# SSD groups of a hybrid decoder layer: the second state product issued behind the products of y, the transposes back to channels moved into the next group

## The chip, the cores and the metric

The kernel runs on one core of one Trainium2 chip. The metric is the device time of one launch in microseconds (us), given as the median of three runs. Besides it there is one profiled execution, and all shares and rows below are of that one. The engines are named as the profile names them: PE (matrix products and transposes), DVE (vector), ACT (activations, scaled copies), POOL, SP (issues most DMAs). The granted clock of PE was 0.997 of full speed, that is the 2.4 GHz level throughout.

## The reference

One decoder layer over 256 tokens and 2048 channels, all in float32. One projection of the input feeds three token mixers (Mamba-2 SSD, S5, RWKV-7), their gates and the merge gates; the branch outputs are projected, gated, summed, projected once more, and normalized. The change is in the SSD mixer, which has 8 groups of 4 heads and two chunks of 128 tokens:

```python
def ssd_chunked(xh, dt, a, bm, cm):
    x = (xh * dt[..., None]).reshape(b, c, l, g, j, p)
    cs = jnp.cumsum(da, -1)
    lmat = jnp.exp(segsum(da))
    cb = jnp.einsum('bclgn,bcsgn->bcgls', cc, bc)
    y_diag = jnp.einsum('bcgls,bgjcls,bcsgjp->bclgjp', cb, lmat, x)
    decay_states = jnp.exp(cs[..., -1:] - cs)
    states = jnp.einsum('bclgn,bgjcl,bclgjp->bcgjpn', bc, decay_states, x)
    ...
    y_off = jnp.einsum('bclgn,bcgjpn,bgjcl->bclgjp', cc, states, jnp.exp(cs))
    return (y_diag + y_off).reshape(b, s, h, p)

# mamba2_branch, after it
    y = ssd_chunked(xh, dt, a, bm, cm) + d_skip[:, None] * xh
    y = y.reshape(b, s, SSD_WIDTH) * jax.nn.silu(z)
    yg = y.reshape(b, s, SSD_GROUPS, SSD_WIDTH // SSD_GROUPS)
    yg = yg * lax.rsqrt(jnp.mean(jnp.square(yg), -1, keepdims=True) + SSD_NORM_EPS)
    return yg.reshape(b, s, SSD_WIDTH) * norm_w
```

## The kernel before

**Matrix products.** Every large product is made of three passes over a split of both operands (high by high, low by high, high by low). Weights come in halves of 512 KB: SP issues the DMA into a raw buffer (tile `raw_*`, ring of 4, line 338), ACT makes the high half (`hi_*`, ring of 4, L344), DVE subtracts it from the raw one (`lo_*`, ring of 4, L346), and PE runs 24 products on it: L417 to L419 in `proj` (tiles `ps_*`, 3 PSUM buffers with tag "pj"), L863 to L865 for the SSD gate z (tiles `zq`, same 3 buffers), L1234 to L1236 for the branch outputs (`br`).

**Order of the work.** The rows of the program are issued group by group from a list: first the RWKV part (to about 545 us), then the second list, which holds the SSD groups S0 to S7 (about 463 to 843 us, overlapping RWKV's last chunks), between them the tiles s0 to s7 of S5, then the splits of the SSD outputs (step "ah", L424 and L425, tiles `yh0h`, `yh0l`), the branch outputs with their gates (`g0_j` is a gate's projection, `b0_j` the weights of the branch product, `sg` the gate, L1281, L1297), and the output projection. This list is only the order in which instructions are created. A scheduler with a timeline model of its own decides the order in each engine's queue, and the pools hand out their buffers in that order. `high_priority` moves what is created under it ahead; `issue_after(ins)` keeps what is created under it behind `ins` in its engine's queue. Each engine then works its queue strictly in order.

**One SSD group.** Four projections give xs (2), B and C; every second group also makes z for two groups (`zs`, one buffer, tanh on L869 and a product on L870). Two DMAs fetch the cumulated decays for all partitions (`csb0`, `csb1`, line 896; the same ring of 5 buffers holds `xdt` and `y_`). PE makes C by B of both chunks and turns B (`cb`, L902, L903) and xs (`xt`, L912). DVE scales (`xdt` L914, `y` L916, `xdec` L921). PE makes the state of the first chunk (`st`, L924), ACT copies it (`ST`, L926), PE multiplies it by C of the second chunk (L927, the second state product), DVE scales that and adds it to y (L929, L930). Meanwhile ACT and DVE make the decay matrices in place in csb (relu L936, exp L937, times CB L938), and PE makes the products of y (`y`, L942). Then comes the chain to the end of the group: sum (L945), times z (L946), squares (L950), root (L952), reciprocal (L953), scaling (L955), four transposes back to channels on PE (`yT`, L959), and the scaled copies into `ya` (ACT, L961). The tiles `cb`, `xt`, `st`, `y` and `yT` of all groups share two PSUM buffers (tag "s"). `ya` lies in memory that RWKV used, so the first four of these copies are written together at 545 us.

Of the kernel before, what the change touches and what calls it, by code (L numbers as in the profile page):

```python
# [11 lines left out]
ALU = mybir.AluOpType  # L12
# [4 lines left out]
T = 256  # L17
# [187 lines left out]
def emit(tc, I, O, parts=("rwkv", "s5", "ssd", "final"), dbg=None):  # L205
    nc = tc.nc
    ctx = ExitStack()
    with ctx:
# [67 lines left out]
        for st in PROG2:  # L276
            k, n = st[0], st[1:]
            if st == "dt":
                ssd_dt(g)
            elif k == "S":  # L280
                ssd_group(g, int(n))
                if st == "S7":
                    sd.close()
                    g.fp = ctx.enter_context(tc.tile_pool(name="fp", bufs=1, reuse_waits="tile"))
            elif k == "s":
                s5_tile(g, int(n))
            elif k == "z":
                s5_zb(g, int(st[2:]))
            elif st == "ch":
                acts[2] = hilo_in(g, "yh2", g.yc, lambda nm: ych.pop(0), g.ycr)  # L290
            elif st == "ah":
                ring = lambda nm: g.fp.tile([128, T], F32R, name=nm, tag="hl", bufs=31)
                acts[0] = hilo_in(g, "yh0", g.ya, ring, g.yar)
            elif st == "bh":
                s5.close()
                g.op = ctx.enter_context(tc.tile_pool(name="op", bufs=1, reuse_waits="tile"))
                out_setup(g)
                acts[1] = hilo(g, "yh1", [g.yb[:, j, :] for j in range(8)], True)
            elif k in "cab":
                branch(g, "abc".index(k), int(n), acts, wts)  # L300
            elif k == "U":
                s5_glu(g)
            elif k == "G":
                gate_b(g, int(n))
# [484 lines left out]
LC = 128  # L789
# [62 lines left out]
def ssd_z(g, zp):  # L852

    nc = g.nc
    ps = [g.pp.tile([128, 512], F32, name=f"zq{zp}_{tk}", tag="pj", bufs=3) for tk in range(2)]
    for kb in range(4):
        hi, lo = g.loadw(g.I["wza"][4 * zp + kb], f"za{zp}_{kb}")
        for k in range(4):
            kk = 4 * kb + k
            f0, l0 = kk == 0, kk == NK - 1  # L860
            for tk in range(2):
                t = slice(128 * tk, 128 * tk + 128)
                nc.tensor.matmul(ps[tk], lhsT=g.xhi[:, kk, t], rhs=hi.k512(k), start=f0, stop=False)  # L863
                nc.tensor.matmul(ps[tk], lhsT=g.xhi[:, kk, t], rhs=lo.k512(k), start=False, stop=False)  # L864
                nc.tensor.matmul(ps[tk], lhsT=g.xlo[:, kk, t], rhs=hi.k512(k), start=False, stop=l0)  # L865
    g.zs = g.cz(f"zs{zp}")
    with g.tc.high_priority():
        for tk in range(2):
            nc.scalar.activation(g.zs[:, tk, :], ps[tk], AF.Tanh, scale=0.5)  # L869
            nc.vector.scalar_tensor_tensor(g.zs[:, tk, :], g.zs[:, tk, :], 1.0, ps[tk], ALU.add, ALU.mult)  # L870


def ssd_group(g, gr):
    nc, tc = g.nc, g.tc
    cv = []
    for n, t in (("xs0", 2 * gr), ("xs1", 2 * gr + 1), ("B", 16 + gr), ("C", 24 + gr)):
        ps = g.proj(f"x{t}")
        a = g.cv(f"{n}_{gr}")
        with tc.high_priority():
            nc.scalar.activation(a, ps, AF.Identity, scale=g.p("cw", 96 + t), bias=g.p("cb", t))  # L880
            for d in (1, 2, 3):
                nc.vector.scalar_tensor_tensor(a[:, d:T], ps[:, 0:T - d], g.p("cw", 32 * (3 - d) + t), a[:, d:T], ALU.mult, ALU.add)
        th = g.kp.tile([128, T], F32, name=f"th{n}_{gr}", tag="th", bufs=2)
        nc.scalar.activation(th, a, AF.Tanh)
        nc.vector.scalar_tensor_tensor(a, th, 1.0, a, ALU.add, ALU.mult)
        cv.append(a)
    if gr % 2 == 0:
        ssd_z(g, gr // 2)
    zs = g.zs[:, :, 256 * (gr % 2):256 * (gr % 2) + 256]
    xs, B, C = cv[0:2], cv[2], cv[3]  # L890
    idn = g.c("ident")
    hs = slice(4 * gr, 4 * gr + 4)
    csb = []
    for c in range(2):
        t = g.k2(f"csb{c}_{gr}", (128, 4, LC))
        nc.sync.dma_start(t, g.csd[hs, LC * c:LC * c + LC].unsqueeze(0).to_broadcast([128, 4, LC]))
        csb.append(t)

    p1 = g.pp.tile([128, 3, LC], F32, name=f"cb{gr}", tag="s", bufs=2)
    for c in range(2):  # L900
        w = slice(LC * c, LC * c + LC)
        nc.tensor.matmul(p1[:, c, :], lhsT=B[:, w], rhs=C[:, w], start=True, stop=True)  # L902
    nc.tensor.transpose(p1[:, 2, :], B[:, 0:LC], idn)  # L903
    BT = g.k1(f"BT{gr}", (128, LC))
    nc.scalar.activation(BT, p1[:, 2, :], AF.Copy)
    CBm = g.k1(f"CBm{gr}", (128, 2, LC))
    nc.vector.tensor_tensor(CBm, p1[:, 0:2, :], g.c("mC").unsqueeze(1).to_broadcast([128, 2, LC]), ALU.mult)

    p2 = g.pp.tile([128, 2, 4, 64], F32, name=f"xt{gr}", tag="s", bufs=2)
    for c in range(2):  # L910
        for q in range(2):
            nc.tensor.transpose(p2[:, c, 2 * q:2 * q + 2, :].rearrange("p a b -> p (a b)"), xs[q][:, LC * c:LC * c + LC], idn)  # L912
    xdt = g.k2(f"xdt{gr}", (128, 2, 4, 64))
    nc.vector.tensor_tensor(xdt, p2, g.csT[:, 1, :, hs].unsqueeze(3).to_broadcast([128, 2, 4, 64]), ALU.mult)  # L914
    y = g.k2(f"y_{gr}", (128, 2, 4, 64))
    nc.vector.tensor_tensor(y, p2, g.dskb[:, hs].unsqueeze(1).unsqueeze(3).to_broadcast([128, 2, 4, 64]), ALU.mult)  # L916
    dec = g.kp.tile([128, 4], F32, name=f"dec{gr}", tag="dec", bufs=2)
    nc.vector.tensor_tensor(dec, csb[0][:, :, LC - 1], g.csT[:, 0, 0, hs], ALU.subtract)
    nc.scalar.activation(dec, dec, AF.Exp)
    xdec = g.k1(f"xdec{gr}", (128, 4, 64))  # L920
    nc.vector.tensor_tensor(xdec, xdt[:, 0], dec.unsqueeze(2).to_broadcast([128, 4, 64]), ALU.mult)  # L921

    p3 = g.pp.tile([128, 2, T], F32, name=f"st{gr}", tag="s", bufs=2)
    nc.tensor.matmul(p3[:, 0, :], lhsT=BT, rhs=xdec.rearrange("p a b -> p (a b)"), start=True, stop=True)  # L924
    ST = g.k1(f"ST{gr}")
    nc.scalar.activation(ST, p3[:, 0, :], AF.Copy)  # L926
    nc.tensor.matmul(p3[:, 1, :], lhsT=C[:, LC:T], rhs=ST, start=True, stop=True)  # L927
    off = g.k1(f"off{gr}", (128, 4, 64))
    nc.vector.tensor_tensor(off, p3[:, 1, :].rearrange("p (a b) -> p a b", a=4), g.ecs[:, hs].unsqueeze(2).to_broadcast([128, 4, 64]), ALU.mult)  # L929
    nc.vector.tensor_tensor(y[:, 1], y[:, 1], off, ALU.add)  # L930

    M = csb
    for c in range(2):
        E = csb[c]
        for h in range(4):
            nc.scalar.activation(E[:, h, :], E[:, h, :], AF.Relu, scale=-1.0, bias=g.csT[:, 0, c, 4 * gr + h:4 * gr + h + 1])  # L936
        nc.scalar.activation(E, E, AF.Exp, scale=-1.0)  # L937
        nc.vector.tensor_tensor(E, E, CBm[:, c, :].unsqueeze(1).to_broadcast([128, 4, LC]), ALU.mult)  # L938
    p4 = g.pp.tile([128, 2, 4, 64], F32, name=f"y{gr}", tag="s", bufs=2)
    for c in range(2):  # L940
        for h in range(4):
            nc.tensor.matmul(p4[:, c, h, :], lhsT=M[c][:, h, :], rhs=xdt[:, c, h, :], start=True, stop=True)  # L942

    y = y.rearrange("p c a b -> p c (a b)")
    nc.vector.tensor_tensor(y, y, p4.rearrange("p c a b -> p c (a b)"), ALU.add)  # L945
    nc.vector.tensor_tensor(y, y, zs, ALU.mult)  # L946
    ss = g.kp.tile([128, 2], F32, name=f"ss{gr}", tag="ss", bufs=2)
    sq = g.k1(f"sq{gr}")
    for c in range(2):
        nc.scalar.activation(sq, y[:, c, :], AF.Square, accum_out=ss[:, c:c + 1])  # L950
    rs = g.kp.tile([128, 2], F32, name=f"rs{gr}", tag="rs", bufs=2)
    nc.scalar.activation(rs, ss, AF.Sqrt, scale=1.0 / 256, bias=g.ssdeps)  # L952
    nc.vector.reciprocal(rs, rs)  # L953
    for c in range(2):
        nc.scalar.activation(y[:, c, :], y[:, c, :], AF.Identity, scale=rs[:, c:c + 1])  # L955
    p6 = g.pp.tile([128, 2, T], F32, name=f"yT{gr}", tag="s", bufs=2)
    for q in range(2):
        for c in range(2):
            nc.tensor.transpose(p6[:, q, LC * c:LC * c + LC], y[:, c, 128 * q:128 * q + 128], idn)  # L959
    for q in range(2):  # L960
        nc.scalar.activation(g.ya[2 * gr + q], p6[:, q, :], AF.Identity, scale=g.p("nw", 2 * gr + q))  # L961

# [427 lines left out]
```

## Time and profile before

| what | value |
|---|---|
| median of 3 runs | 1308.43 us (1305.89 to 1310.21) |
| profiled execution | 1302.54 us, its span 1300.6 us |
| granted clock of PE | 0.997 |
| PE busy | 1268.7 us (98%) |
| DVE busy | 995.7 us (77%) |
| ACT busy | 768.5 us (59%) |
| bytes moved | 230.71 MB, 177 GB/s |

The span is the time from the first to the last instruction of the profiled execution; 1.9 us of its run lie outside. A wait is idle time of an engine just before an instruction, put down to what released it. Where PE is busy nearly all the time, what it waits for is what can be gained, and every new wait of PE is lost.

### The profile page before, as it was taken

The page shows a single profiled execution, that of the slowest core. Times are in us where ns is not written, and L with a number is a line of the kernel's source. Part 1 is how long each engine was busy: PE and PEld are TensorE (multiplying, and loading weights), DVE is VectorE, ACT ScalarE, POOL GpSimd, SP SyncE. Part 2 cuts the span into 40 slices and gives each one's busy share as a digit, 9 for nine tenths or more (in the row PEclk, how much of TensorE's full clock was granted, in tenths as well). Part 3 has the DMA queues.
Part 4 walks back from the last instruction along what each step waited for, and adds up shares of the span by engine and source line. Part 5 has one row for each costly group of instructions (what it writes and reads, how often), then busy time and mean ns, then how long its engine had stood idle before and what let it go on. Part 6 is the DMA issues. An engine that isn't in the chain of part 4 may idle for free.

```text
span 1300.6 us, 27378 instructions
## 1 busy us (share of the span) xinstructions
PE 1268.7 (98%) x10916; PEld 1195.2 (92%) x10916; DVE 995.7 (77%) x1823; ACT 768.5 (59%) x1379; POOL 14.8 (1%) x72
## 2 busy tenths in 40 slices
PE   8999999999999999989999999999999999999996
PEld 8999999999989889889989989999999999999885
DVE  6779987669959857889999867999597565448655
ACT  6676555577555657885756766766454454444530
POOL 2000000000000000000000000000000000000000
PEclk9999999999999999999999999999999999999998
DMA  8655655444564554555555556456655656677751
GB/s 313 181 169 173 187 174 167 139 124 145 166 177 152 168 183 132 159 186 164 178 163 180 170 178 195 146 158 192 193 171 164 193 179 211 209 230 243 255 167 65
DMA packets 97039, 230.71 MB, mean 177 GB/s; under 512 B 26736, under 2 KB 41616, under 8 KB 96912
## 3 DMA queue, kind: packets, MB, share of 16 engines
q1 hardware_dynamic: 96336, 227.60, 57.1%
q8 instruction: 86, 1.41, 0.5%
q10 hardware_dynamic: 576, 1.36, 0.3%
q14 instruction: 41, 0.34, 0.1%
HBM read 224.37 MB, written 3.24 MB: 175 GB/s over the span
## 4 chain that ended last, share of the span: by engine, by line
PE 80%; DVE 7%; ACT 6%; DMA 3%; issue 2%; SPq 1%; DVEq 0%; POOL 0%; ACTq 0%; POOLq 0%
PE ps_g L418 6%; PE ps_g L417 6%; PE ps_g L419 6%; PE br L1235 4%; PE br L1234 4%; PE br L1236 4%; PE ps_x L417 3%; PE ps_x L418 3%; PE ps_x L419 3%; PE po L1337 2%; PE po L1338 2%; PE po L1339 2%; PE zq L865 2%; PE zq L864 2%; PE zq L863 2%
## 5 line engine op out<-in xcount | busy, mean ns | idle before, releaser
L417 PE MATMUL ps_g<-xhi,hi_g 128*128 128x256 f32 x768 | 215.2, 280 | 0.0
L418 PE MATMUL ps_g<-xlo,hi_g 128*128 128x256 f32 x768 | 215.1, 280 | 0.0
L419 PE MATMUL ps_g<-xhi,lo_g 128*128 128x256 f32 x768 | 213.8, 278 | 0.0
L346 DVE TENSOR_TENSOR lo_g<-raw_g,hi_g 128x1024 fp32r<-128x1024 f32 x96 | 117.5, 1224 | 66.6 <-ACT hi_g L344 61.9
L344 ACT ACTIVATE hi_g<-raw_g 128x1024 fp32r<-128x1024 f32 x96 | 101.5, 1058 | 93.8 <-PE ps_g L418 71.4
L418 PEld LDWEIGHTS ps_g<-xlo,hi_g 128*128 128x128 f32 x768 | 144.6, 188 | 2.0 <-issue 1.0
L417 PEld LDWEIGHTS ps_g<-xhi,hi_g 128*128 128x128 f32 x768 | 144.6, 188 | 0.9
L417 PE MATMUL ps_x<-xhi,hi_x 128*128 128x256 f32 x512 | 144.6, 282 | 0.6 <-ACT sq L950 0.6
L419 PEld LDWEIGHTS ps_g<-xhi,lo_g 128*128 128x128 f32 x768 | 144.2, 188 | 0.5
L418 PE MATMUL ps_x<-xlo,hi_x 128*128 128x256 f32 x512 | 143.9, 281 | 0.0
L419 PE MATMUL ps_x<-xhi,lo_x 128*128 128x256 f32 x512 | 143.6, 280 | 0.0
L344 ACT ACTIVATE hi_b<-raw_b 128x1024 fp32r<-128x1024 f32 x64 | 67.8, 1059 | 75.8 <-PE br L1235 43.9
L346 DVE TENSOR_TENSOR lo_x<-raw_x,hi_x 128x1024 fp32r<-128x1024 f32 x64 | 78.3, 1223 | 27.1 <-ACT hi_x L344 27.1
L417 PEld LDWEIGHTS ps_x<-xhi,hi_x 128*128 128x128 f32 x512 | 96.3, 188 | 1.6 <-ACT sq L950 0.8
L419 PEld LDWEIGHTS ps_x<-xhi,lo_x 128*128 128x128 f32 x512 | 96.3, 188 | 0.9 <-issue 0.2
L418 PEld LDWEIGHTS ps_x<-xlo,hi_x 128*128 128x128 f32 x512 | 96.3, 188 | 0.7 <-issue 0.2
L346 DVE TENSOR_TENSOR lo_b<-raw_b,hi_b 128x1024 fp32r<-128x1024 f32 x64 | 78.8, 1231 | 21.6 <-ACT hi_b L344 19.6
L344 ACT ACTIVATE hi_x<-raw_x 128x1024 fp32r<-128x1024 f32 x64 | 67.5, 1055 | 39.7 <-PE ps_x L418 23.2
L1234 PE MATMUL br<-yh0h,hi_b 128*128 128x256 f32 x256 | 72.0, 281 | 0.7 <-DVE sg L1297 0.7
L1235 PE MATMUL br<-yh0l,hi_b 128*128 128x256 f32 x256 | 72.3, 283 | 0.0
L1236 PE MATMUL br<-yh0h,lo_b 128*128 128x256 f32 x256 | 71.7, 280 | 0.0
L676 DVE TENSOR_TENSOR Pm<-TT,AT 128x16 f32<-128x16 f32 (+30 forms) x124 | 50.8, 410 | 11.6 <-POOL AT L672 5.8
(446 smaller groups left out, 3872.9 us busy)
## 6 DMA issues: line engine op xcount, KB each, us to landing
raw_g<-in_wt SPq DMA_DIRECT2D x96, 512.0 KB, 4.4
raw_x<-in_wt SPq DMA_DIRECT2D x64, 512.0 KB, 4.2
raw_za<-in_wza SPq DMA_DIRECT2D x32, 512.0 KB, 3.8
raw_b<-in_wba SPq DMA_DIRECT2D x32, 512.0 KB, 4.5
raw_wo<-in_wout SPq DMA_DIRECT2D x32, 512.0 KB, 4.7
raw_k<-in_wt SPq DMA_DIRECT2D x16, 512.0 KB, 4.8
raw_r<-in_wt SPq DMA_DIRECT2D x16, 512.0 KB, 4.1
raw_v<-in_wt SPq DMA_DIRECT2D x16, 512.0 KB, 3.8
```

The lines of the kernel that those rows point to most:

```text
L344: nc.scalar.activation(hi, raw, AF.Copy)
L346: nc.vector.tensor_tensor(lo, raw, hi.bitcast(F32), ALU.subtract)
L417: m.append(nc.tensor.matmul(ps, lhsT=hi.k(k), rhs=g.xhi[:, k, :], start=(k == 0), stop=False))
L418: m.append(nc.tensor.matmul(ps, lhsT=hi.k(k), rhs=g.xlo[:, k, :], start=False, stop=False))
L419: m.append(nc.tensor.matmul(ps, lhsT=lo.k(k), rhs=g.xhi[:, k, :], start=False, stop=(k == NK - 1)))
L676: nc.vector.tensor_tensor(Pm[:, :, 0:n], TT[:, :, 0:n], col, ALU.mult)
L863: nc.tensor.matmul(ps[tk], lhsT=g.xhi[:, kk, t], rhs=hi.k512(k), start=f0, stop=False)
L864: nc.tensor.matmul(ps[tk], lhsT=g.xhi[:, kk, t], rhs=lo.k512(k), start=False, stop=False)
L865: nc.tensor.matmul(ps[tk], lhsT=g.xlo[:, kk, t], rhs=hi.k512(k), start=False, stop=l0)
L1234: nc.tensor.matmul(ps, lhsT=hi.k(k0 + k), rhs=h, start=(k == 0), stop=False)
L1235: nc.tensor.matmul(ps, lhsT=hi.k(k0 + k), rhs=l, start=False, stop=False)
L1236: nc.tensor.matmul(ps, lhsT=lo.k(k0 + k), rhs=h, start=False, stop=(k == n - 1))
```

## The change

The second state product and the two DVE steps after it are created after the products of y, and the product is kept behind the last of them in PE's queue. The transposes back to channels, with the copies into `ya`, become a function of their own, `ssd_back`. Groups 0 to 6 store it, and the next group calls it right after its transpose of B is created; its transposes are kept behind that instruction in PE's queue. Group 7 calls it at once.

```diff
-    nc.tensor.transpose(p1[:, 2, :], B[:, 0:LC], idn)
+    m = nc.tensor.transpose(p1[:, 2, :], B[:, 0:LC], idn)
+    if gr:
+        g.late(m.ins)
     BT = g.k1(f"BT{gr}", (128, LC))
...
     ST = g.k1(f"ST{gr}")
     nc.scalar.activation(ST, p3[:, 0, :], AF.Copy)
-    nc.tensor.matmul(p3[:, 1, :], lhsT=C[:, LC:T], rhs=ST, start=True, stop=True)
-    off = g.k1(f"off{gr}", (128, 4, 64))
-    nc.vector.tensor_tensor(off, p3[:, 1, :].rearrange("p (a b) -> p a b", a=4), g.ecs[:, hs].unsqueeze(2).to_broadcast([128, 4, 64]), ALU.mult)
-    nc.vector.tensor_tensor(y[:, 1], y[:, 1], off, ALU.add)
...
     for c in range(2):
         for h in range(4):
-            nc.tensor.matmul(p4[:, c, h, :], lhsT=M[c][:, h, :], rhs=xdt[:, c, h, :], start=True, stop=True)
+            my = nc.tensor.matmul(p4[:, c, h, :], lhsT=M[c][:, h, :], rhs=xdt[:, c, h, :], start=True, stop=True)
+    with tc.issue_after(my.ins):
+        nc.tensor.matmul(p3[:, 1, :], lhsT=C[:, LC:T], rhs=ST, start=True, stop=True)
+    off = g.k1(f"off{gr}", (128, 4, 64))
+    nc.vector.tensor_tensor(off, p3[:, 1, :].rearrange("p (a b) -> p a b", a=4), g.ecs[:, hs].unsqueeze(2).to_broadcast([128, 4, 64]), ALU.mult)
+    nc.vector.tensor_tensor(y[:, 1], y[:, 1], off, ALU.add)
...
     for c in range(2):
         nc.scalar.activation(y[:, c, :], y[:, c, :], AF.Identity, scale=rs[:, c:c + 1])
+    if gr < 7:
+        g.late = lambda m: ssd_back(g, gr, y, m)
+    else:
+        ssd_back(g, gr, y, None)
+
+
+def ssd_back(g, gr, y, m):
+    nc, idn = g.nc, g.c("ident")
     p6 = g.pp.tile([128, 2, T], F32, name=f"yT{gr}", tag="s", bufs=2)
-    for q in range(2):
-        for c in range(2):
-            nc.tensor.transpose(p6[:, q, LC * c:LC * c + LC], y[:, c, 128 * q:128 * q + 128], idn)
+    with g.tc.issue_after(m) if m is not None else ExitStack():
+        for q in range(2):
+            for c in range(2):
+                nc.tensor.transpose(p6[:, q, LC * c:LC * c + LC], y[:, c, 128 * q:128 * q + 128], idn)
```

The first place is PE's queue at the end of group 5. In the queue before, the transposes of y of group 5 (L959) stand in the middle of the products for z of groups 6 and 7:

```order
L864 MATMUL zq3_0_9819<-lo_za3_2_0_9897,xhi_69 128x512
L959 MATMUL yT5_9536<-cst_220,y_5_9489 128x128
L865 MATMUL zq3_0_9819<-hi_za3_2_0_9895,xlo_70 128x512
L959 MATMUL yT5_9536<-cst_220,y_5_9489 128x128 x3
L863 MATMUL zq3_1_9820<-hi_za3_2_0_9895,xhi_69 128x512
```

In the changed queue they (now L971) stand behind the last of those products and behind C by B of group 6:

```order
L865 MATMUL zq3_1_9813<-hi_za3_3_1_9930,xlo_70 128x512
L902 MATMUL cb6_9967<-C_6_9804,B_6_9735 128x128 x2
L903 MATMUL cb6_9967<-cst_220,B_6_9735 128x128
L971 MATMUL yT5_9971<-cst_220,y_5_9489 128x128 x4
L417 MATMUL ps_zb4_10048<-xhi_69,hi_zb4_0_10038 128x256
```

The four transposes moved back by 46 products of zq3. Those of groups 3, 4 and 6 likewise stand just behind L903 of the next group.

The second place is PE's queue at group 1. Before, its products of y (L942) stand at the start of the products for z of groups 2 and 3, and the second state product (L927) further ahead still:

```order
L744 MATMUL chy3_5216<-MTr7_4088,SVA3_3793 64x64 x2
L747 MATMUL chy3_5216<-XS7_4046,Sz0_280 64x64 x2
L863 MATMUL zq1_1_7148<-hi_za1_0_0_7151,xhi_69 128x512
L942 MATMUL y1_6844<-xdt1_6815,csb0_1_6798 128x64 x4
L942 MATMUL y1_6844<-xdt1_6815,csb1_1_6800 128x64 x4
L864 MATMUL zq1_1_7148<-lo_za1_0_0_7153,xhi_69 128x512
L865 MATMUL zq1_1_7148<-hi_za1_0_0_7151,xlo_70 128x512
```

In the changed queue the products of y (now L940) and the second state product (now L942) stand behind all of zq1, in the projection x6:

```order
L863 MATMUL zq1_1_7141<-hi_za1_3_1_7258,xhi_69 128x512
L864 MATMUL zq1_1_7141<-lo_za1_3_1_7260,xhi_69 128x512
L865 MATMUL zq1_1_7141<-hi_za1_3_1_7258,xlo_70 128x512
L417 MATMUL ps_x6_7376<-xhi_69,hi_x6_0_7366 128x256
L418 MATMUL ps_x6_7376<-xlo_70,hi_x6_0_7366 128x256
L940 MATMUL y1_6840<-xdt1_6815,csb0_1_6791 128x64 x4
L940 MATMUL y1_6840<-xdt1_6815,csb1_1_6793 128x64 x4
L942 MATMUL st1_6824<-ST1_6826,C_1_6783 128x256
```

They moved back past the rest of zq1. The buffer of csb0_1, which these products read, is the one that csb1_2 is loaded into.

The third place is ACT's queue at the tanh of z of groups 2 and 3 (zs1, L869). Before:

```order
L344 ACTIVATE hi_x7_0_7442<-raw_x7_0_7440 128x1024
L869 ACTIVATE zs1_7293<-zq1_0_7147 128x512
L869 ACTIVATE zs1_7293<-zq1_1_7148 128x512
L344 ACTIVATE hi_x7_1_7448<-raw_x7_1_7446 128x1024
L905 ACTIVATE BT2_7306<-cb2_7302 128x128
L344 ACTIVATE hi_x19_0_7511<-raw_x19_0_7509 128x1024
```

In the changed queue (L934 is the relu on csb, L1035 to L1037 are sines of S5's setup):

```order
L344 ACTIVATE hi_x7_0_7435<-raw_x7_0_7433 128x1024
L344 ACTIVATE hi_x7_1_7441<-raw_x7_1_7439 128x1024
L1035 ACT_TABLE_LOAD
L1035 ACTIVATE s5t_0_5813<-s5t_0_5813 128x32
L1036 ACTIVATE s5t_0_5813<-s5t_0_5813 128x32
L1037 ACTIVATE s5t_0_5813<-s5t_0_5813,hpi_5829 128x32
L934 ACTIVATE csb1_2_7293<-csb1_2_7293,csT_5994 128x128 x4
L344 ACTIVATE hi_x19_0_7504<-raw_x19_0_7502 128x1024
L869 ACT_TABLE_LOAD
L869 ACTIVATE zs1_7286<-zq1_0_7140 128x512
L869 ACTIVATE zs1_7286<-zq1_1_7141 128x512
```

The tanh now stands behind the sines, the relu on csb1_2, a weight half and a table load. The projection x7 is written into the PSUM buffer of zq1_0.

The fourth place is DVE's queue ahead of the low half of the gate's weights g0_1, after the last SSD group. Before:

```order
L346 TENSOR_TENSOR lo_b0_5_1_11417<-raw_b0_5_1_11413,hi_b0_5_1_11415 128x1024
L1188 TENSOR_TENSOR s5t4_1_10779<-s5t4_2_10780,s5S4_10732 128x512
L425 TENSOR_TENSOR yh0l11_11135<-ya11_5947,yh0h11_11134 128x256
L1190 TENSOR_TENSOR s5t4_0_10778<-s5t4_0_10778,s5C4_10731 128x512
L346 TENSOR_TENSOR lo_g0_1_0_11628<-raw_g0_1_0_11624,hi_g0_1_0_11626 128x1024
```

In the changed queue (lines 12 higher):

```order
L346 TENSOR_TENSOR lo_b0_5_1_11417<-raw_b0_5_1_11413,hi_b0_5_1_11415 128x1024
L1142 SCALAR_TENSOR_TENSOR s5cq5_11484<-s5tb5_1_11491 128x128
L425 TENSOR_TENSOR yh0l7_11119<-ya7_5943,yh0h7_11118 128x256
L1174 SCALAR_TENSOR_TENSOR s5C5_11521<-s5C5_11521,s5pw_5834,s5x5_1_6_11540 128x64
L1173 SCALAR_TENSOR_TENSOR s5S5_11522<-s5C5_11521,s5pw_5834,s5x5_1_6_11540 128x64
L1174 SCALAR_TENSOR_TENSOR s5C5_11521<-s5C5_11521,s5pw_5834,s5x5_2_5_11545 128x32
L1173 SCALAR_TENSOR_TENSOR s5S5_11522<-s5C5_11521,s5pw_5834,s5x5_2_5_11545 128x32
L425 TENSOR_TENSOR ybgl4_13777<-yb_237,ybgh4_13776 128x256
L1132 TENSOR_TENSOR s5tb5_2_11496<-s5cq5_11484,s5lr_5877 128x256
L1133 TENSOR_TENSOR s5tb5_2_11496<-s5cq5_11484,s5li_5878 128x256
L425 TENSOR_TENSOR yh0l8_11123<-ya8_5944,yh0h8_11122 128x256
L346 TENSOR_TENSOR lo_g0_1_0_11628<-raw_g0_1_0_11624,hi_g0_1_0_11626 128x1024
```

Work of S5's tile 5 (s5C5, s5S5, s5tb5), which stood behind this half, now stands ahead of it. Over the whole of DVE's queue, what is ahead of it in the changed kernel and not before: 3 operations of 128x512, 8 of 128x256, 4 of 128x128 and 10 of 128x64 or 128x32; the other way round, 3 of 128x256 (L425).

## Rows read from the trace of the kernel before

**Rows 1.** The page's busy times: us, share of the span, instructions.

```profile
PE 1268.7 (98%) x10916; PEld 1195.2 (92%) x10916; DVE 995.7 (77%) x1823; ACT 768.5 (59%) x1379; POOL 14.8 (1%) x72
```

**Rows 2.** Waits of PE: who waited for whom, us in total, times, longest.

```profile
PE yT L959 <- ACT y L955: 4.1, 5, 1.3
...
PE st L927 <- ACT ST L926: 2.7, 1, 2.7
...
PE br L1234 <- DVE B L882: 1.3, 1, 1.3
PE br L1234 <- DVE acc L1295: 1.1, 1, 1.1
PE br L1234 <- DVE sg L1297: 0.7, 1, 0.7
```

**Rows 3.** Timeline of PE: start, duration, instruction, [idle before <- releaser].

```profile
505.32 0.28 PE L419 MATMUL ps_x<-xhi,lo_x 128*128 128x256 f32 x1
...
506.68 0.28 PE L419 MATMUL ps_x<-xhi,lo_x 128*128 128x256 f32 x1
508.09 0.33 PE L959 MATMUL yT<-cst,y 128*128 128x128 f32 x1 [1.13 <-ACT y L955]
...
566.32 0.70 PE L927 MATMUL st<-ST,C 128*128 128x256 f32 x2 [2.71 <-ACT ST L926]
...
584.00 0.55 PE L959 MATMUL yT<-cst,y 128*128 128x128 f32 x3 [0.50 <-ACT y L955]
```

**Rows 4.** Timeline of ACT, table load ahead of the state's copy.

```profile
564.07 1.28 ACT L937 ACT_TABLE_LOAD   x1
```

**Rows 5.** Chain that ended last, pieces in order of time: start, duration, what.

```profile
494.06 0.43 PE st L927 x2
...
494.61 0.85 PE y L942 x8
495.48 4.54 DMA csb<-csd
...
744.28 4.95 DMA csb<-csd
```

**Rows 6.** Timeline of ACT at the end of group 0 and at zs1.

```profile
500.10 1.28 ACT L936 ACTIVATE csb<-csb,csT 128x128 f32<-128x128 f32 x4 [3.15 <-DMA csb<-csd]
501.29 1.04 ACT L344 ACTIVATE hi_x<-raw_x 128x1024 fp32r<-128x1024 f32 x1
...
504.18 0.31 ACT L761 ACTIVATE Sz<-SVA 64x128 f32<-64x128 f32 x1
504.51 1.28 ACT L952 ACT_TABLE_LOAD   x1
505.80 0.29 ACT L952 ACTIVATE rs<-ss,ssdeps 128x2 f32<-128x2 f32 x1
...
551.25 1.29 ACT L869 ACTIVATE zs<-zq 128x512 f32<-128x512 f32 x2 [0.95 <-PE zq L865]
```

**Rows 7.** Timeline of DVE, product of zs.

```profile
552.73 0.68 DVE L870 SCALAR_TENSOR_TENSOR zs<-zs,zq 128x512 f32<-128x512 f32 x1
```

**Rows 8.** Windows: length, then busy us of PE, PEld, DVE, ACT, POOL, clock, DMA.

```profile
556.00:600.00 44.00, 38.36 (x321) 37.34 (x320) 40.30 (x124) 33.87 (x61) 0.21 (x2) 1.00 0.53 168
836.00:850.00 14.00, 14.00 (x140) 13.46 (x138) 11.88 (x34) 13.85 (x37) 0.21 (x2) 1.00 0.59 164
```

**Rows 9.** Timeline of DVE around the low half of g0_1.

```profile
864.96 1.22 DVE L346 TENSOR_TENSOR lo_g<-raw_g,hi_g 128x1024 fp32r<-128x1024 f32 x1
866.10 0.69 DVE L1191 TENSOR_TENSOR s5t<-s5t,s5C 128x512 f32<-128x512 f32 x1
866.70 0.42 DVE L425 TENSOR_TENSOR yh0l<-ya,yh0h 128x256 fp32r<-128x256 f32 x1
...
872.84 0.29 DVE L1162 SCALAR_TENSOR_TENSOR s5C<-s5C,s5pw,s5x 128x64 f32<-128x64 f32 x1
```

**Rows 10.** Timeline of PE, the first product with that low half.

```profile
866.24 0.38 PE L419 MATMUL ps_g<-xhi,lo_g 128*128 128x256 f32 x1
```

## The prediction

> **What bounds the kernel now.** I read the page's busy times first: PE is busy for 1268.7 of 1300.6 us [rows 1]. All idle time of PE is therefore 31.9 us, and nothing can be gained but there, since the change neither adds nor removes an operation of PE. Next the waits of PE [rows 2]: the reader is to see which of them belong to the instructions moved. The transposes of y (L959) wait for ACT's scaling (L955) five times, 4.1 us together; the second state product (L927) waits once, 2.7 us. That makes 6.8 us, 0.52% of the span, the most that the edits can give by their own waits. Then the timeline of PE, to see to which group each wait belongs [rows 3]: group 0 has 1.13 us at 508.09, group 2 has 0.50 us at 584.00 and also the state product's 2.71 us at 566.32. So groups 4, 5 and 6 hold 4.1 - 1.13 - 0.50 = 2.5 us. Last I read the queues of the changed kernel against these, because SSD groups share two PSUM buffers, one zs and five csb buffers with their neighbours, so a step made later frees its buffer later.
>
> A measurement of this kernel can tell about 0.3% (3.9 us) from no change. The gain in view is not far above that.
>
> **Part 1, transposes of groups 4 to 6: -2.5 us.** In the changed queue they stand behind C by B of the next group, as the first place of the change shows for group 5, where 46 more products for z stand ahead. The spacing of such products is at least that of the 128x256 ones, (506.68 - 505.32) / 12 = 0.113 us [rows 3], so even at that price 46 make 5.2 us, more than the longest of these waits, 1.3 us [rows 2]. If the cover goes, the old wait comes back, at most 2.5 us.
>
> **Part 2, second state product of group 2: -2.7 us.** ACT's copy ST was late there because table loads for S5's sines and for exp stood ahead of it; the last of them is at 564.07 [rows 4]. In the changed queue of ACT the three sines of S5's setup stand together, well ahead (third place), and the product itself stands behind the products of y. I take all 2.7 us as gone. What is late next: the sum with y on DVE, which nothing on PE needs until the next group.
>
> **Part 3, group 0: +0.2 us.** Its transposes keep nearly the same place on PE. What they wait for is a chain that the change leaves alone: the products of y end at 495.46, only then the next group's csb can be loaded, 4.54 us [rows 5], ACT waits 3.15 us for it at its relu [rows 6], and squares and root stand behind that in ACT's queue. One more small operation (0.3 us, the second Sz) now stands ahead of the scaling. The 1.13 us stay, plus 0 to 0.5.
>
> **Part 4, a new wait behind z of groups 2 and 3: +2.9 us.** Products of y of group 1 moved past zq1 (second place), so csb1_2 can be fetched only after them, and the relu on it stands ahead of the tanh of zs1 in ACT's queue (third place). That tanh and the product behind it free the PSUM buffer that projection x7 needs. From the end of the first four products of y: DMA 4.5 us (4.54; 4.95 elsewhere) [rows 5]; four relus 1.2, a weight half 0.95 (start of the next operation after each), a table load 1.28, the first tanh 0.6 (half of 1.29) [rows 6]; the product with zs 0.68 [rows 7]. Sum 9.3 us. Beside it PE has the other four products of y (half of 0.85) and the second state product, 0.43 [rows 5], 46 products of x6 by 0.113 (5.2) [rows 3] and three small ones of cb2 (0.3): 6.4 us. So PE waits 2.9 us ahead of x7. Before, the tanh followed zq at once (0.95 us idle of ACT, then 551.25) [rows 6], and nothing waited. Bounds: 0, if the scheduler's order turns out looser because x6 itself is late on PE; 4.5, if the DMA takes 4.95 and a low weight half of 1.22 us [rows 9] stands ahead of the product with zs. I take the worked-out value.
>
> The Trainium skill bears on the table load. The row shows 1.28 us for the load at 504.51, with 0.02 us between the end of the operation ahead and its start, and the activation behind it starts 1.29 us later [rows 6]. The page "ScalarE: Activation LUTs", section "What ACT_TABLE_LOAD costs", says that each switch of tables costs the load of some 1283 ns and a drain of about 1380 ns besides. By that this part would be an estimated +4.3 us in place of +2.9. The trace agrees with the load and shows no drain of that size, so the row's price stands.
>
> **Part 5, 556 to 600 us: +1.3 us.** Here DVE is the tight engine, busy 40.3 of 44 us [rows 8]; three waits of PE hang on it or follow it: 1.3 and 1.1 us [rows 2], 0.50 us [rows 3]. The 2.7 us of part 2 lie just ahead. PE arriving earlier finds DVE no further; and in the changed queue DVE has 2 to 3 us more work ahead of the weight halves of the RWKV branch than before. DVE's 3.7 idle us of the stretch can take up part. From below -1 (the 0.50 and one more wait go), from above +3 (all the added work counts); I take the middle.
>
> **Part 6, the stretch behind group 7: +3.5 us.** Group 7's end comes some 4 us later in the queues, the splits of ya move behind it, and the scheduler fills DVE's queue with S5's tile 5 (fourth place). Ahead of the low half of g0_1 come 25 operations, and 3 leave. One of 128x512 takes 0.60 us to the next, one with 0.42 us of its own about 0.33, one of 64 columns some 0.2 (they overlap by the 0.09 us that the first two rows show) [rows 9]: 3 x 0.60 + 8 x 0.33 + 14 x 0.2 - 3 x 0.33 = 6.2 us. That half had no lead: it was ready at 866.18 [rows 9], and PE used it at 866.24 [rows 10]. Of the 6.2 us, the idle of DVE from 836 to 850, 14 - 11.9 = 2.1 us [rows 8], can take up its share; leaves 4.1. I take 3.5, since the wait for sg of 0.7 us [rows 2] a little later on the same engine is swallowed by it. Bounds: 0 (the moved work was ready to run in idle slots further ahead) and 6.2.
>
> **Sum.** -2.5 - 2.7 + 0.2 + 2.9 + 1.3 + 3.5 = +2.7 us. Behind some 960 us the queues are the same again, and PE has no waits there, so the sum reaches the end as it is. Against the profiled execution: 1302.54 + 2.7 = 1305.2. That execution lies 5.9 us below the median of the runs; by the median it is 1308.43 + 2.7 = 1311.1, and I forecast 1311.
>
> **Rivals.** *The gain comes and the new waits do not* (faster): parts 1 and 2 give 5.2 us, parts 4 to 6 together cost under 1.3. For it: both price lists of new waits rest on orders, and queues that look late often have slack from DVE's idle time (77% busy over the span [rows 1]). Against it: the half at 866.24 had 0.06 us of lead. Time 1308.4 - 5.2 = 1303.2, and 1301.6 if all of 6.8 us go.
>
> *DVE's late low halves decide* (slower): in the stretch from 850 us on, S5's tile 5 ahead of the low halves costs its whole 6.2 us. From 4.7 us there on the sum passes +3.9. For it: the missing lead; against it: 2.1 idle us just before. Time 1308.4 - 0.8 (parts 1 to 5) + 6.2 = 1313.8; with part 4 at 4.5, 1315.4.
>
> *The change doesn't do what it says for the transposes*: they still wait, now at the next group's start, because the chain (squares, root, two table loads) has been queued behind more of ACT's other work. Then part 1 falls away: +2.7 + 2.5 = +5.2, 1313.6. Against it: the distance of group 5 grew by 5.2 us and more, where 1.3 were missing.
>
> **How the numbers follow.** The forecast, between -3.9 and +3.9 us of the median, 0.43; the faster rival 0.22; DVE's late halves 0.28; transposes that still wait 0.07. So faster 0.22, same 0.43, slower 0.35. The range: down to the faster rival with most of its gain, 1302.5; up to the slower one with its upper price and 2 us of doubt on part 5, 1317.5. The forecast's own range is 1304.5 to 1312.3.
>
> **What would show it.** In the waits of PE: yT for y falls from 4.1 to about 1.3 us, one time or two, the longest at about 508; the state product's wait on ST is gone; a new wait of ps_x of about 3 us near 552 to 556, released by DVE's product on L870; waits of ps_g on low halves or of br on DVE's sg between 850 and 885 us that sum to 3 or 4. If x7 starts without a wait, part 4 is wrong; if PE is busy throughout 850 to 900, part 6 is; if yT of groups 4 to 6 waits on, part 1 is. The forecast falls if the new waits sum to under 1 or over 10 us.

## The result, and the profile after

| | before | after |
|---|---|---|
| median, four runs each | 1308.57 us (1305.89 to 1310.21) | 1315.97 us (1315.32 to 1319.35) |
| profiled execution, its span | 1302.54, 1300.6 | 1316.38, 1314.6 |
| granted clock of PE | 0.997 | 0.989 |

The change makes the kernel slower: the ratio is 1.0064 [1.004, 1.0088]. Timed again beside other kernels (e5 below) it was 1.009 [1.0078, 1.0102]. The time lies inside the range, but it is the slower rival that came in, not the likeliest case.

The page's busy times of the changed kernel, which answer to [rows 1]:

```profile
PE 1279.6 (97%) x10916; PEld 1206.1 (92%) x10916; DVE 996.3 (76%) x1823; ACT 770.2 (59%) x1381; POOL 14.8 (1%) x72
```

PE is busy for 10.9 us more with the same 10916 instructions. So a part of the loss is no wait at all: some products took longer. The waits of PE, which answer to [rows 2]:

```profile
PE br L1247 <- DVE yh0l L425: 4.1, 3, 2.5
PE ps_x L417 <- DVE zs L870: 3.6, 1, 3.6
...
PE br L1246 <- DVE B L882: 1.5, 1, 1.5
PE ps_g L419 <- DVE lo_g L346: 1.5, 1, 1.5
PE yT L971 <- ACT y L958: 1.1, 1, 1.1
```

Of the waits that the edits aimed at, only group 0's transposes are left. New are 3.6 us ahead of projection x7 and, at the end, 4.1 us on the low halves of SSD's own outputs (`yh0l`, the step "ah") and 1.5 us on a low half of gate weights. PE's timeline shows what follows the first of them (start, duration, instruction, idle before):

```profile
565.05 0.39 PE L417 MATMUL ps_x<-xhi,hi_x 128*128 128x256 f32 x1 [3.65 <-DVE zs L870]
565.27 0.28 PE L418 MATMUL ps_x<-xlo,hi_x 128*128 128x256 f32 x1
565.39 0.28 PE L419 MATMUL ps_x<-xhi,lo_x 128*128 128x256 f32 x1
...
565.89 0.41 PE L419 MATMUL ps_x<-xhi,lo_x 128*128 128x256 f32 x1
566.11 0.41 PE L417 MATMUL ps_x<-xhi,hi_x 128*128 128x256 f32 x1
```

The first products start 0.12 us apart, those after 565.7 are 0.21 us apart. Fifteen products go like that, to 568.67, at 1.36 us more than at the spacing of 0.1165 us that is usual in these traces. The same is seen twice behind group 7:

```profile
856.54 0.39 PE L1247 MATMUL br<-yh0l,hi_b 128*128 128x256 f32 x1 [1.17 <-DVE yh0l L425]
...
858.08 0.39 PE L1247 MATMUL br<-yh0l,hi_b 128*128 128x256 f32 x1 [0.38 <-DVE yh0l L425]
...
860.15 0.58 PE L419 MATMUL ps_g<-xhi,lo_g 128*128 128x256 f32 x1 [1.45 <-DVE lo_g L346]
860.53 0.41 PE L417 MATMUL ps_g<-xhi,hi_g 128*128 128x256 f32 x1
860.75 0.41 PE L418 MATMUL ps_g<-xlo,hi_g 128*128 128x256 f32 x1
...
890.27 0.58 PE L1247 MATMUL br<-yh0l,hi_b 128*128 128x256 f32 x1 [2.53 <-DVE yh0l L425]
890.65 0.41 PE L1248 MATMUL br<-yh0h,lo_b 128*128 128x256 f32 x1
...
892.00 0.58 PE L417 MATMUL ps_g<-xhi,hi_g 128*128 128x256 f32 x1 [0.51 <-ACT hi_g L344]
```

From 860.15 on 26 products run so, 2.6 us more than usual, and from 890.27 on 24, 2.7 us more beside the wait of 0.51. The windows of the changed kernel (length, then busy us of PE, PEld, DVE, ACT, POOL, granted clock, DMA) say why:

```profile
550.00:600.00 50.00, 44.86 (x368) 43.48 (x367) 45.85 (x140) 35.39 (x71) 0.21 (x2) 0.97 0.52 163
850.00:900.00 50.00, 43.87 (x354) 40.94 (x357) 47.54 (x104) 29.61 (x72) 0.42 (x4) 0.86 0.45 131
857.00:862.00 5.00, 3.12 (x15) 2.56 (x14) 5.00 (x9) 3.83 (x11) 0.10 (x1) 0.71 0.18 29
862.00:867.00 5.00, 5.00 (x30) 5.00 (x29) 5.00 (x14) 1.96 (x5) 0.00 (x0) 0.61 0.56 184
890.00:895.00 5.00, 4.22 (x18) 3.93 (x19) 5.00 (x10) 4.03 (x8) 0.10 (x1) 0.50 0.10 41
```

Having stood still, PE was granted half its clock for some us (0.50 in the last window, the 1.2 GHz level). In the kernel before, the same 50 us read:

```profile
850.00:900.00 50.00, 49.32 (x454) 47.70 (x453) 49.41 (x97) 29.33 (x59) 0.42 (x4) 1.00 0.59 179
```

The count says most: 454 products before, 354 after. DVE is nearly full in both (49.4 and 47.5 of 50 us), so what changed is mainly the order of its work. DVE's timeline at the place of [rows 9], in the changed kernel:

```profile
853.50 0.42 DVE L425 TENSOR_TENSOR yh0l<-ya,yh0h 128x256 fp32r<-128x256 f32 x1
853.84 2.33 DVE L1196 TENSOR_TENSOR_SCAN s5t<-s5m,s5t 128x512 f32<-128x512 f32 x2
856.09 0.40 DVE L425 TENSOR_TENSOR yh0l<-ya,yh0h 128x256 fp32r<-128x256 f32 x1
856.40 0.69 DVE L1201 TENSOR_TENSOR s5t<-s5t,s5S 128x512 f32<-128x512 f32 x1
857.00 0.68 DVE L1200 TENSOR_TENSOR s5t<-s5t,s5S 128x512 f32<-128x512 f32 x1
857.61 0.42 DVE L425 TENSOR_TENSOR yh0l<-ya,yh0h 128x256 fp32r<-128x256 f32 x1
...
887.57 2.33 DVE L1196 TENSOR_TENSOR_SCAN s5t<-s5m,s5t 128x512 f32<-128x512 f32 x2
889.82 0.40 DVE L425 TENSOR_TENSOR yh0l<-ya,yh0h 128x256 fp32r<-128x256 f32 x1
```

Single splits stand between scans and products of S5, and PE waits for three of them: the one of 856.09 lets PE go on at 856.54, that of 889.82 at 890.27. In DVE's queue before, ten of the 16 splits stand ahead of the scans of S5's tile 4 (tile `s5t`, here 853.84) and all ahead of tile 5's (887.57); in the changed queue two, and all but the last.

**Where the time went.** I compared the starts of PE's instructions in the two traces at equal amounts of PE work done (worked out from the starts, after minus before). At 462 us, before the change acts, the difference is +2.75 us: RWKV's part differs that much from run to run. From there to 843 us it is -0.1, from 843 to 925 us +11.4, and behind that nothing. Of the 11.4 us, 5.4 are waits between 850 and 900 us (1.17, 0.38, 1.45, 2.53 and 0.51 make 6.0; PE idled 0.7 there before), 5.3 are the two spells at half clock, and 0.7 are pauses I did not assign.

### The profile page after: what moved, and what is told of

Its sections match the earlier page's. It is cut to its first block, busy times and chain, and to the rows that moved or that the text cites. A ratio compares the mean times of both kernels' runs of the same rounds, so it can differ in the third digit from the quotient of the medians.

```text
span 1314.6 us, 27379 instructions
## 1 busy us (share of the span) xinstructions
PE 1279.6 (97%) x10916; PEld 1206.1 (92%) x10916; DVE 996.3 (76%) x1823; ACT 770.2 (59%) x1381; POOL 14.8 (1%) x72
## 3 DMA queue, kind: packets, MB, share of 16 engines
q10 hardware_dynamic: 576, 1.36, 0.3%
## 4 chain that ended last, share of the span: by engine, by line
PE 85%; DVE 5%; ACT 4%; DMA 3%; issue 2%; SPq 1%; DVEq 0%; POOL 0%; ACTq 0%; POOLq 0%
PE ps_g L418 7%; PE ps_g L417 6%; PE ps_g L419 6%; PE br L1247 5%; PE br L1246 4%; PE br L1248 4%; PE ps_x L417 4%; PE ps_x L418 4%; PE ps_x L419 4%; PE po L1351 2%; PE po L1350 2%; PE po L1349 2%; PE zq L864 2%; PE zq L865 2%; PE zq L863 2%
```

## Experiments

Apart from e4, all kernels are the changed one: as it is (e5), with some parts put back, or with a few lines more. Two sets say which groups have which part: LATE, the groups whose transposes move into the next group, and SECOND, those whose second product stands behind the products of y. LATE 0 to 6 with SECOND 0 to 7 is the changed kernel, and both empty is before. As a diff against the changed kernel (e1's sets; `second` is the second state product, `second_dve` its two DVE steps):

```diff
-    if gr:
+    if gr - 1 in (0, 1, 2, 3, 4, 5, ):
         g.late(m.ins)
...
+    if gr not in (0, 1, 2, 3, 4, 5, 6, ):
+        second()
+        second_dve()
...
-    with tc.issue_after(my.ins):
-        nc.tensor.matmul(p3[:, 1, :], lhsT=C[:, LC:T], rhs=ST, start=True, stop=True)
...
+    if gr in (0, 1, 2, 3, 4, 5, 6, ):
+        with tc.issue_after(my.ins):
+            second()
+        second_dve()
...
-    if gr < 7:
+    if gr in (0, 1, 2, 3, 4, 5, ):
         g.late = lambda m: ssd_back(g, gr, y, m)
```

Ratios are to the kernel before on the same chip, with 95% intervals.

**e1, the end of the SSD part as before** (the diff above).

> The changed kernel, except that group 6's transposes of y are issued at once, as before the change, and group 7's second state product stands where it stood. On the engines' queues everything up to group 6 is as in the changed kernel, and the stretch behind group 7 as in the kernel before. Theory A (the loss lies behind group 7: the low halves of the SSD outputs come late on DVE, PE waits, and its clock is halved after each wait): PE busy at least 49 of 50 us from 850 to 900, granted clock 1.00 there; about 11 us less than the changed kernel's profile in that stretch; against the kernel before a ratio of 0.997 to 1.002, with the wait ahead of projection x7 still about 3.6 us. Theory B (the loss is the wait ahead of x7 and what it drags along): nothing of it goes, ratio 1.004 to 1.007.

Measured 1306.18 us, 1.0012 [0.9998, 1.0025]. The end is as before:

```profile
850.00:900.00 50.00, 49.09 (x452) 47.20 (x451) 48.62 (x98) 29.92 (x63) 0.42 (x4) 1.00 0.58 178
```

The wait ahead of x7 stays (4.4 us, and 1.5 us at half clock behind it). So the stretch behind group 7 carries most of the loss.

**e2, the second product alone**: LATE empty, SECOND 0 to 7.

> Only the second state product is moved behind the products of y, in all groups; the transposes of y stay in their group. In the queues y's products of group 1 still stand behind zq1, and the tanh of zs1 behind the relu on csb1_2; the stretch behind group 7 is as before. Theory A: waits of the transposes of groups 4 to 6 as before (2.5 us), the wait of the state product (2.7 us) gone, a wait of 3 to 4.5 us ahead of x7 with 2 to 4 us at half clock behind it, and nothing lost behind 850 us: ratio 1.000 to 1.003. Theory B: ratio 1.004 to 1.007.

Measured 1311.04 us, 1.0049 [1.0032, 1.0066]: more than expected. Its end is whole (PE busy 49.32 of 50 us), but the wait ahead of x7 is there, at 5.5 us, and 1.6 us at half clock behind it. That wait needs no late transposes, then. The ratio lies in the range of Theory B, and nearly all that this trace loses against before lies ahead of 850 us: beside the wait for x7 a branch product waits 3.1 us for B at 593.56 us (before: 1.3 us, once).

**e3, late transposes of groups 4 to 6 alone**: LATE 4 to 6, SECOND empty.

> Only the transposes of y of groups 4, 5 and 6 are moved into the next group; the second state product is created where it was. The queues up to group 4 are as before, and the stretch behind group 7 nearly so. Theory A: their waits (2.5 us) go, nothing new comes: ratio 0.997 to 0.9995, the state product's 2.7 us at about 566 still there. Rival: late transposes of group 6 alone make the splits of the outputs late: PE busy under 47 of 50 us from 850 to 900, clock under 0.95 there, ratio 1.002 to 1.006.

Measured 1305.12 us, 1.001 [0.9995, 1.0026]: a miss. Their waits are gone, yet nothing is gained; small new waits (1.0 on S5's outputs, 0.8 twice on weight halves) came in their place. In the trace there is also half clock behind the state product's wait: that wait is 2.8 us here and in e4, but the granted clock from 566 to 571 us is 0.66 here and 1.00 in e4.

**e4, the kernel before, once more**, for how far one trace repeats.

> The kernel before, unchanged, for a second trace of it. Theory A: PE busy at least 49 of 50 us and clock 1.00 from 850 to 900, as in the first trace, and the first 450 us within 3 us of either trace. Theory C (the stretch behind 850 us varies from run to run whatever the queues): waits of several us and a lower clock there in this trace too.

Measured 1303.29 us, the same waits (`yT` 5.1, `st` 2.8). From 450 us on its PE took 0.9 us more than in the first trace; differences of that size between traces say nothing.

**e5, the changed kernel, once more.**

> The changed kernel, unchanged, beside the next one on the same chip. All theories: the same waits as in its first trace (3.6 us ahead of x7, 1.1 us of group 0's transposes, some 6 us from 855 to 893), granted clock 0.5 for 5 to 6 us behind each of the two waits near 860 and 890; ratio to before 1.004 to 1.009.

Measured 1316.07 us, 1.009 [1.0078, 1.0102]. The chief lines repeat:

```profile
PE ps_x L417 <- DVE zs L870: 4.4, 1, 4.4
PE br L1247 <- DVE yh0l L425: 4.1, 3, 2.5
...
850.00:900.00 50.00, 43.88 (x350) 40.80 (x348) 47.26 (x104) 30.10 (x71) 0.42 (x4) 0.86 0.45 131
```

**e6, the changed kernel with PE kept at work in its late waits.** 46 products that nobody reads stand in front of products with `yh0l`, written into the other half of the PSUM buffer:

```diff
-        nc.tensor.matmul(ps, lhsT=hi.k(k0 + k), rhs=h, start=(k == 0), stop=False)
+        m = nc.tensor.matmul(ps, lhsT=hi.k(k0 + k), rhs=h, start=(k == 0), stop=False)
+        for _ in range(fill.get(k, 0)):
+            with g.tc.high_priority(), g.tc.issue_after(m.ins):
+                m = nc.tensor.matmul(junk, lhsT=g.xhi[:, 0, 0:128], rhs=g.xlo[:, 0, :], start=False, stop=False)
...
+    fill = {7: {2: 9, 4: 15}, 5: {15: 22}}.get(j, {}) if br == 0 else {}
```

> The changed kernel with 46 products more on PE, whose result nobody reads, put into the places where PE waits behind group 7: 9 and 15 in front of the waits near 856 and 860 us, 22 in front of the one near 890 us (0.118 us each, 5.4 us). Elsewhere the queues of PE are as in the changed kernel. Theory D (about half of what is lost behind 850 us is the clock that falls after PE has stood still): the products take the place of the waits, the granted clock stays 1.00 from 850 to 900, and 4 to 6 us come back although there is more work: ratio to before 1.000 to 1.004. Rival E (the clock falls for another reason, or the fall costs nothing since PE waits for DVE there anyway): ratio as the changed kernel's, 1.004 to 1.009, or higher by up to 5 us if the products come on top.

```profile
850.00:900.00 50.00, 48.17 (x448) 44.48 (x447) 48.64 (x107) 32.23 (x76) 0.42 (x4) 1.00 0.44 133
```

The clock stays at 1.00, and from the first product of SSD's branch to the end PE takes 445.7 us, against 449.4 (after) and 449.9 (e5): some 4 us come back although 5.4 us of work were added. So in the traces of this stretch half clock costs time by itself; the medians don't settle it. The median, 1314.12 us, 1.0077 [1.0058, 1.0097], is above what I expected, and its interval overlaps e5's: the splits are nearly as late as in the changed kernel (33.7 us against 35.8 in the table below), and this trace lost 2.4 us at half clock behind the wait for x7 (1.4 in the changed kernel).

**e7, e1 with the relu behind the tanh.** Part 4 says that the relu on csb1_2 keeps the tanh of zs1 waiting on ACT:

```diff
-            nc.scalar.activation(g.zs[:, tk, :], ps[tk], AF.Tanh, scale=0.5)
+            g.zt = nc.scalar.activation(g.zs[:, tk, :], ps[tk], AF.Tanh, scale=0.5)
...
+            with tc.issue_after(g.zt.ins) if gr == 2 and c == 1 else ExitStack():
...
```

> As the run with the old tail (groups 0 to 5 with late transposes, 0 to 6 with the late second product), and the four relus on csb1_2 are kept behind the tanh of zs1 on ACT. Theory A: the wait ahead of x7 (4.4 us there) and the half clock behind it go, and no wait of more than 1.5 us takes its place from 545 to 600 us: ratio to before 0.995 to 0.999, faster than both kernels. Rival: y's products of group 2 now come late on PE and it waits at them or at the state product: ratio 1.000 to 1.003.

Measured 1300.67 us, 0.9974 [0.9962, 0.9985], faster than before. The wait ahead of x7 fell from 4.4 to 0.4 us, the half clock behind it is gone. 1306.18 - 1300.67 = 5.5 us for one order on ACT, against 4.4 - 0.4 + 1.5 = 5.5 by the rows. The two medians come from two chips; by the ratios to before it is 0.0038, or 5.0 us.

**e8, late transposes alone**: LATE 0 to 6, SECOND empty.

> Only the transposes of y are moved into the next group, for groups 0 to 6; the second state product is created where it was. In the queues zs1's tanh stands as before, and group 7's end and S5's tile 5 stand nearly as late as in the changed kernel. Theory A: no wait ahead of x7; behind 850 us PE waits 2 to 8 us for low halves, with half clock after waits of 2 us and more; ratio to before 1.001 to 1.006. If the second product is the part that makes the end late, nothing is lost behind 850 us: ratio 0.996 to 0.999.

Measured 1298.87 us, 0.9961 [0.9949, 0.9972], the lowest median of all (e9's interval below is nearly the same). Theory A had expected a loss; the other case came in. The wait of `st` on ST is gone although that product was put back; no wait for x7; PE is busy 49.16 of 50 us from 850 on.

**e9, the changed kernel with one instruction put back**: LATE 0 to 6, SECOND all but group 1. The instruction is group 1's second product (its two DVE steps go with it); after e8 I took it that it alone carries the loss.

> The changed kernel with one thing put back: in group 1 the second state product is created ahead of the products of y, as before the change; all other groups keep both parts. Theory F (two PSUM buffers: with both parts, the state's buffer is held until the products of y are done, and these need the other buffer, which the last group's late transposes hold until they are copied out; in group 1 that copy can't be written before 545 us, so y's products move behind zq1 and everything late in the changed kernel follows from that order): no wait ahead of x7, PE busy at least 48.5 of 50 us from 850 to 900 with clock 1.00; ratio to before 0.995 to 0.998. Rival (each of the eight late second products costs its share): ratio 1.004 to 1.009, an eighth less than the changed kernel.

Measured 1300.74 us, 0.9964 [0.9949, 0.9979]. Both losses are gone:

```profile
850.00:900.00 50.00, 49.16 (x452) 47.51 (x451) 44.42 (x92) 31.54 (x65) 0.31 (x3) 1.00 0.59 179
```

In its queue of PE the products of y of group 1 stand in x26, ahead of all of zq1 (in the trace from 524.48 us on, with zq1 from 531.87); the second place of the change shows them behind zq1 in the changed kernel:

```
L417 MATMUL ps_x26_7083<-xhi_69,hi_x26_0_7073 128x256
L951 MATMUL y1_6844<-xdt1_6815,csb0_1_6791 128x64 x4
L951 MATMUL y1_6844<-xdt1_6815,csb1_1_6793 128x64 x4
```

**e10, that one instruction alone beside the transposes**: LATE 0 to 6, SECOND group 1.

> The counterpart: transposes of groups 0 to 6 moved as in the changed kernel, and the second state product moved in group 1 alone. In the queues y's products of group 1 stand behind zq1 and the tanh of zs1 behind the relus on csb1_2, and their exp too; the stretch behind group 7 stands as in the kernel before. Theory F: the wait ahead of x7 comes back, 4 to 6 us, with 1 to 4 us of half clock behind it, and nothing is lost behind 850 us: 5 to 9 us more than with late transposes alone, ratio to before 0.999 to 1.003. If the group is not what matters: as late transposes alone, 0.995 to 0.998.

Measured 1308.9 us, 1.0026 [1.0014, 1.0037]. Against e8 that is 0.65% for one instruction. The wait is

```profile
565.26 0.58 PE L417 MATMUL ps_x<-xhi,hi_x 128*128 128x256 f32 x1 [5.80 <-DVE zs L870]
```

and 24 products behind it at half clock cost 2.4 us more: 8.2 of the 10 us (1308.9 - 1298.87; the two ran beside different runs of before). The end lost a little (PE busy 47.23 of 50 us, one wait of 1.0 on `yh0l`); the rest of the changed kernel's loss there comes only with the other second products.

**e11, the transposes in another set of PSUM buffers.** If y1 is late because `yT0` holds one of the two shared buffers, other buffers should free it:

```diff
-    p6 = g.pp.tile([128, 2, T], F32, name=f"yT{gr}", tag="s", bufs=2)
+    p6 = g.pp.tile([128, 2, T], F32, name=f"yT{gr}", tag="pj", bufs=3)
```

> The changed kernel with the transposes back to channels written into the three PSUM buffers of the projections (tag pj) instead of the two of the SSD groups. Both parts of the change stay. In the queues y's products of group 1 stand ahead of zq1, and the transposes of group 7 some 290 rows earlier on PE. Theory F: the buffers were the reason, so no wait ahead of x7, no wait above 1 us for low halves of the SSD outputs behind 850 us, clock 1.00: ratio to before 0.993 to 0.999. Rival: the projections now wait for their buffers (held until 545 us by group 0's transposes): waits of ps_x or zq of 3 us and more, ratio above 1.002.

Measured 1349.64 us, 1.0336 [1.0316, 1.0356]. The wait for x7 is gone, but the projections now share their buffers with the transposes:

```profile
PE cb L902 <- DVE C L885: 9.2, 1, 9.2
PE ps_x L417 <- DVE xs L882: 7.6, 1, 7.6
PE s5pk L1155 <- ACT s5WT L1151: 7.6, 3, 3.5
PE st L926 <- DVE xdec L923: 5.6, 1, 5.6
```

The products of y of group 1 run at 511.56 us, well ahead of zq1 (544.68), as the theory wants it. But the order shifted everywhere, so this doesn't settle the question of the buffer.

**e12, late transposes without group 0**: LATE 1 to 6, SECOND empty.

> Late transposes alone, for groups 1 to 6 (group 0 as before, since nothing is gained there), the second state product created where it was. Theory F: as with late transposes for 0 to 6, no wait ahead of x7 and none above 1.5 us behind 850 us; three table loads of ACT fewer than before in the queue: ratio to before 0.994 to 0.998. Rival: the order happens to be worse somewhere, ratio 0.998 to 1.002.

Measured 1307.74 us, 1.0017 [1.0004, 1.0029]: a miss, 0.56% above e8. A wait of 5.2 us of a branch product at 593 us, with 2.2 us at half clock behind it, has come in. Why group 0's late transposes prevent it I did not find out.

## Why the prediction was right or wrong

**The runs together.** The wait for x7 by DVE's product of zs (3.6 to 5.8 us) is there in the changed kernel, e1, e2, e5, e6 and e10, all with group 1's second product late. It is missing, or 0.4 us, in before, e3, e4, e8, e9 and e12, where it is not late, in e7, where the tanh no longer stands behind the relu, and in e11, where y1 runs early. For the end, the lateness of the splits goes with the time, both from the first product of SSD's branch, worked out from the starts in the traces:

| us from that product to | before | e1 | e8 | e9 | e10 | e6 | after | e5 |
|---|---|---|---|---|---|---|---|---|
| end of the last `yh0l` | 22.9 | 23.5 | 14.8 | 14.9 | 26.7 | 33.7 | 35.8 | 35.9 |
| start of the last product of all | 438.3 | 438.2 | 435.6 | 435.7 | 440.8 | 445.7 | 449.4 | 449.9 |

e2, e3, e4, e7 and e12 lie near before and e1: 22.9 to 25.1 us and 437.7 to 439.7 us. In e11 the splits end before that product starts.

**The number** fell inside the range partly by luck. The upper end, 1317.5 us, counts 9.1 us from the median of before, while the traces differ by 11.3 us behind 462 us (-0.1 + 11.4). The medians differ by 7.4 us only (1315.97 - 1308.57) because before's four runs took longer there than its later ones: those, on two chips, have medians of 1304.84, 1304.83 and 1305.06 us, and beside the second of them the changed kernel is 11.2 us slower (1316.07, e5).

**Parts 1 to 3** held: the waits of groups 4 to 6 and the 2.7 us of the state product are gone, and group 0's stays, at 511.08, with its 1.13 us (1.9 in e5). What the prediction did not see is that these 5.2 us need only a part of the edits: e8 loses the state product's wait without touching that product.

**Part 4** held in its place and its chain; its size was low. The chain of waits of the changed kernel shows each term (start, duration, what):

```profile
554.40 5.65 DMA csb<-csd
...
560.14 1.28 ACT csb L934 x4
561.42 0.95 ACT hi_x L344
...
562.38 1.28 ACT L869
...
563.68 0.60 ACT zs L869
...
564.31 0.70 DVE zs L870
```

All terms but the DMA are within 0.1 us of their price. The DMA took 5.65 us for 4.5, and PE's cover was 7.0 us (554.40 to 565.05 less 3.65) for 6.4, hence 3.65 for 2.9. The table load stands 0.02 us behind the operation ahead and the tanh 1.30 us after its start. The Trainium skill's page "ScalarE: Activation LUTs", section "What ACT_TABLE_LOAD costs", adds a drain of about 1380 ns to a load. No gap of that size is seen here either. What was left out altogether is the half clock behind the wait, 1.4 us. With it the part is 5.0 us; e7, which takes the same wait away from e1, gains about as much.

**Part 5** was too high. The stretch held the wait on B (1.5, 1.3 before) and lost the rest: parts 1 to 5 together measured -0.1, and -2.5 - 2.7 + 3.65 + 1.4 make -0.15 without it. So it was about 0 for +1.3.

**Part 6** is the step that failed: 11.4 us for +3.5, and above its upper bound of 6.2. Its mechanism, S5's work ahead of the splits and low halves in DVE's queue, is what the traces show (scans and products of tiles 4 and 5), and e1 takes it away. Two things were mis-sized. It priced one late half of the gate's weights (g0_1), while PE waits at five places, three of them for splits that S5's scans, 2.33 us for two, have passed in the queue. And it charged a wait at its length, where PE's clock was halved behind two of them as well, 5.3 us more. So the slower rival was right in kind, "from 4.7 us there on", and given too small a chance.

**Which part of the edit caused it** was in none of the steps. The two losses lie 300 us apart, yet putting one instruction's place back removes both (e9), and they come apart in e1 and e10. For the first the way is shown: y1 behind zq1, csb1_2 late, the tanh late, x7 without a buffer. That group 1's product pushes y1 back because its PSUM buffer is then held until y1 is done, while `yT0` holds the other until `ya` may be written (546.91 us), is argued from the queues only. Two runs fit it without proving it: in e2 y1 is late without any late transposes, at 552.75 us, behind group 0's copies into `ya` (549.00 us), and in e11, with `yT0` elsewhere, it is early. How the scheduler comes from there to another order of DVE's queue behind group 7 stays open.

## What to carry to other kernels

Price a new wait of a matrix engine that is always busy at its length and, beside it, at the chance of a spell at half clock. Here such a spell cost 1.4 to 2.7 us; behind some waits it came (2.53 us in the changed kernel, 2.96 in e9), behind others not (2.71 in before, 2.96 in e8, 3.14 in e2). Where a scheduler sets the order and buffers are shared, apply an edit group by group: here a single group turned a gain of 0.4% (e9) into a loss of 0.6 to 0.9%. Late transposes alone (e8) beat both kernels, 1298.87 us, but leaving out group 0's took that gain away again (e12).

## What the runs showed of the hardware

A wait of the same length at the same place halved the clock in one run and not in another. In e8 and e9 it is the wait of 2.96 us for B. PE's first product after it, and its clock in the window around it, in e8 (first fence) and e9:

```profile
586.96 0.36 PE L1256 MATMUL br<-ych,hi_b 128*128 128x256 f32 x1 [2.96 <-DVE B L882]
...
585.00:590.00 5.00, 3.04 (x26) 3.07 (x27) 5.00 (x13) 3.77 (x7) 0.00 (x0) 1.00 0.63 204
```

```profile
586.25 0.55 PE L1256 MATMUL br<-ych,hi_b 128*128 128x256 f32 x1 [2.96 <-DVE B L882]
...
585.00:590.00 5.00, 3.75 (x17) 3.78 (x18) 5.00 (x15) 3.00 (x5) 0.00 (x0) 0.52 0.54 180
```

e9 then ran 26 products at 0.21 us apart, 2.6 us more, and e8 none. These are two kernels, but two traces of one kernel differ in the same way. In RWKV's part PE waits 1.80 us for ACT; the changed kernel (first fence) and e5, the same program:

```profile
297.73 0.33 PE L744 MATMUL chy<-MTr,SVA 128*64 128x64 f32 x2 [1.80 <-ACT SVA L737]
...
299.00:303.00 4.00, 4.00 (x22) 4.00 (x23) 3.44 (x10) 3.03 (x5) 0.00 (x0) 0.57 0.17 25
```

```profile
297.61 0.33 PE L744 MATMUL chy<-MTr,SVA 128*64 128x64 f32 x2 [1.80 <-ACT SVA L737]
...
299.00:303.00 4.00, 4.00 (x36) 4.00 (x36) 3.44 (x10) 2.80 (x5) 0.00 (x0) 1.00 0.14 33
```

So the price of such a wait is not fixed, and a single trace shows one draw of it. Nor need it be one long wait: in the changed kernel three waits of 1.17, 0.38 and 1.45 us within 5 us ended at half clock.
